# A norm and split emitted one output unit earlier, with its sum of squares pinned

## The chip, the cores and the metric

The kernel runs on one core of one Trainium2 chip. A core has a matrix engine (TensorE, PE in the profile; its weight loads are PEld), a vector engine (VectorE, DVE), a scalar engine for activations (ScalarE, ACT), GpSimd (POOL) and a queue engine that starts most transfers (SyncE, SP). Each engine works through its own queue in order, and engines wait for one another by semaphores. PE writes to eight accumulation banks (PSUM), which DVE and ACT read. The metric is the device time of one execution in microseconds.

## The reference

One inference step of a decoder trunk of one layer: a half-step SwiGLU feed-forward block, a mixer, a second such block, and a final norm, with plain residual adds. The input is one prompt of 512 tokens and 8 single new tokens of other sequences with saved state, each of 1024 features. The part around the change is the end of the mixer:

```python
y = y + d_skip[:, None] * xs_h
y = y.reshape(b, T, SSD_DIM) * jax.nn.silu(z)
yg = y.reshape(b, T, SSD_GROUPS, SSD_DIM // SSD_GROUPS)      # 2 groups of 512
yg = yg * lax.rsqrt(jnp.mean(yg * yg, axis=-1, keepdims=True) + EPS)
y = yg.reshape(b, T, SSD_DIM) * ssd_norm
cat = jnp.concatenate([pool_out, y], axis=-1)                # 512 + 1024
return cat @ w_out, ...
```

For the 8 new tokens, `y` also holds the product of the saved state with C, which comes from the sample stage below. The result of `cat @ w_out` is added to `h`, which feeds the norm and the gate and up projections of the second feed-forward block.

## The kernel before

Features lie on the 128 partitions, tokens along the free dimension: 520 of them (512 and 8), in two halves of 260. A big product is made of three matmuls for each tile of 128 features (`mm3`, L116 to L119): weight and input are each split into a rounded part (hi) and the rest (lo), and hi x hi, hi x lo and lo x hi are summed in a bank. The split of weights is a cast on ACT (L107, tile `whi`) and a subtraction on DVE (L108, tile `wlo`), three buffers each.

The mixer's order of emission is written out by hand in three strings, `CONV_PLAN`, `GATE_PLAN` and `LAST_PLAN`; each token names a stage and its argument. A planner then lays the emitted instructions out on the engines' queues: an instruction emitted earlier has the higher priority, but a later one may be put ahead of it where the planner holds the earlier one not ready. `tc.keep_in_program_order(x)` forbids one such move: `x` may not be put ahead of the instruction emitted just before it on the same engine. Buffers come from tags: all tiles of one tag share a fixed number of buffers. In the mixer all accumulation banks have one tag (`bank`, L76, eight buffers).

The stages that matter here, all in `mixer`:

- `s` (`sample`, L789): state product of one sequence and one group; loads two tiles through SP, then four products on DVE (L796, tile `junk`), kept in program order. There are 16.
- `G` (`gate`, L932): for group g, finishes the new tokens' part (L803, L804, L940), and multiplies `X` by the activated gate into `zs` (L942, four passes on DVE).
- `H` (`gate_out`, L944): the norm and split of group g. Four squares on ACT (L948, from `zs` into `X`), a sum over the features on PE by a matrix of ones (`rstd`, L158: four accumulating calls of L161 for each half of the tokens, tiles `psr_y{g}0` and `psr_y{g}1`, each in its bank), Sqrt on ACT (L162) and reciprocal on DVE (L163) for each half into `yr`; then four times a product on DVE (L955), a scaled copy on ACT (L956, hi part of `catg`) and a pass on DVE (L957, lo part).
- `o`, `g`, `h` (`wout`, L918): output units for the pooled input (`catp`), the first gate group (`cats[0]`) and the second (`cats[1]`). A unit is one weight load and split, 48 matmuls into four banks (12 each) and four evacuations on DVE that add to `h` (L926). Each letter has four units, 0 to 3.

Before the change H1 is emitted behind g1, the second unit of the first group; its product, `cats[1]`, is first read by h0, which is emitted behind g3. In the text H1, g0 to g3 and h0 stand for these stages.

An L161 call multiplies full fp32 numbers and shows as two PE instructions in the trace.

Of the kernel before, what the change touches and what calls it, by code (L numbers as in the profile page):

```python
# [41 lines left out]
)  # L42
GATE_PLAN = (
    "A4 z0 B3 z1 m3 z2 B4 z3 s2 A5 z4 s2 B5 A6 z5 s2 s2 G0 z6 A7 z7 B6 s2 o0 H0 s2 o1 B7 s2 o2 s2 G1 "
    "o3 g0 g1 H1 g2 g3"
)
LAST_PLAN = "h0 h2 h1 n0 h3 n1 n2 n3"
SAMPLE_U = 3 + SEQ
# [14 lines left out]
def tile_trunk_step(ctx: ExitStack, tc: tile.TileContext, ins: dict, outs: dict):  # L63
    nc = tc.nc

    def pool(name, side, **kw):
        return tc.alloc_tile_pool(name=name, bufs=1, side=side, reuse_waits="tile", **kw)
# [6 lines left out]
    ps = [None]  # L74

    def bank(name):  # L76
        return ps[0].tile([P, 512], F32, tag="ps", name=name)
# [8 lines left out]
    ones = cst.tile([P, P], F32, tag="ones", name="ones")  # L86
# [68 lines left out]
        nc.scalar.activation(out=sq, in_=h[:, d], func=AF.Square)  # L155
        nc.vector.tensor_tensor(out=nx[2], in0=nx[2], in1=sq, op=ALU.add)

    def rstd(r, acc, hs, width, name):  # L158
        ps = bank(f"psr_{name}")[:, : hs.stop - hs.start]
        for k, sq in enumerate(acc):  # L160
            nc.tensor.matmul(ps, ones, sq, start=k == 0, stop=k == len(acc) - 1)  # L161
        nc.scalar.activation(out=r[:, hs], in_=ps, func=AF.Sqrt, bias=eps, scale=1.0 / width)  # L162
        nc.vector.reciprocal(out=r[:, hs], in_=r[:, hs])  # L163

    def rstds(nx, name):
        for b, hs in enumerate(HALVES):
            rstd(nx[3], [nx[2][:, hs]], hs, D, f"{name}{b}")
# [270 lines left out]
    wx1, g1 = pool("wx1", "right"), pool("g1", "right")  # L438
# [4 lines left out]
    for j in range(KD // 2):  # L443
        for d in (j, j + KD // 2):
            q = slice(NVEC + d * NT if d else 0, NVEC + (d + 1) * NT)
# [62 lines left out]
    g2 = f2["ffn"].gp = pool("g2", "left")  # L508
# [52 lines left out]
def mixer(tc, ins, outs, e):  # L561
    nc = tc.nc
    cst, act, wp, tmp, dr, pool = (e[x] for x in ("cst", "act", "wp", "tmp", "dr", "pool"))
    ones = e["ones"]
    bank, load_unit, mm3, ws, v, rstd, rstds, vec, h, nx2, raw_tile, open_f2, fin, fill = (
        e[x] for x in ("bank", "load_unit", "mm3", "ws", "v", "rstd", "rstds", "vec", "h", "nx2", "raw_tile",
                       "open_f2", "fin", "fill"))
    xh, xl, _, r = nx2[0]
# [18 lines left out]
    X = mp.tile([P, NX, NT], F32, tag="X", name="X")  # L587
# [356 lines left out]
    def gate_out(g):  # L944
        zs = zbox[0]
        ry = mp.tile([P, NT], F32, tag="wph", name=f"yr{g}")
        for q in range(4):
            nc.scalar.activation(out=X[:, 4 * g + q], in_=zs[:, 4 * g + q], func=AF.Square)  # L948
        for b, hs in enumerate(HALVES):
            rstd(ry, [X[:, 4 * g + q, hs] for q in range(4)], hs, 512, f"y{g}{b}")  # L950
        cat = cats[g] = xa.tile([P, 2, 4, NT], F32R, tag="xa", bufs=2, name=f"catg{g}")
        for q in range(4):
            i = 4 * g + q
            gn = v("ssd_norm", i)
            nc.vector.tensor_tensor(out=zs[:, i], in0=zs[:, i], in1=ry, op=ALU.mult)  # L955
            nc.scalar.activation(out=cat[:, 0, q], in_=zs[:, i], func=AF.Copy, scale=gn)  # L956
            nc.vector.scalar_tensor_tensor(out=cat[:, 1, q], in0=zs[:, i], scalar=gn, in1=cat[:, 0, q].bitcast(F32),  # L957
                                           op0=ALU.mult, op1=ALU.subtract)
# [13 lines left out]
    def outs_a():  # L972
# [19 lines left out]
        "o": lambda j: wout(catp, 0, j),  # L992
        "G": gate,
        "H": gate_out,
        "g": lambda j: wout(cats[0], 1, j),
        "h": lambda j: wout(cats[1], 2, j, fin),
# [103 lines left out]
```

## Time and profile before

| what | value |
|---|---|
| median of 3 runs | 1002.59 us (1002.44 to 1002.99) |
| profiled execution, its own time | 1003.51 us |
| its span, first to last instruction | 1000.5 us |
| granted PE clock, mean over the span | 0.994 |
| g0 and g1 on PE (96 matmuls, `wo<-catg`) | 571.8 to 583.5 us |
| the four squares of group 1 on ACT (L948) | from 584.34, 2.61 us |
| calls of L161 for group 1 on PE | 585.03 to 591.3 us |
| first matmul of h0 on PE | 600.4 us |

Times in the trace are microseconds from the start of the span. A row of the timeline has start, duration, engine, line, operation, output tile and inputs, shapes and a count of merged instructions; in brackets, for how long the engine sat idle before it and which instruction ended that. In the list of waits, a row names the waiting engine, tile and line, whom it waited for, and the total, the number of times and the longest. Matmuls overlap by pipelining: their duration (0.28 us for 260 columns) is more than their distance in time (0.12 us).

### The profile page before, as it was taken

To read this page: it belongs to the slowest core of one execution; us is meant where nothing else is said; L and a number is where in the kernel's file an instruction comes from. 1 tells how busy PE (TensorE), PEld (TensorE's weight loads), DVE (VectorE), ACT (ScalarE), POOL (GpSimd) and SP (SyncE) were. 2 spreads that over 40 slices of the span, in tenths; PEclk is the share of its full clock that TensorE was granted. 3 is DMA by queue.
4 is the path that set the end of the run, shared out by engine and by line. 5 is a ranking of instruction groups with operands and counts; after the bars stand their busy time and mean duration, and the time that the engine had idled before them with its cause. 6 is when DMAs were issued, how large, how long until landed. Compare 5 with 4: busy or idle time off the path is not lost.

```text
span 1000.5 us, 19362 instructions
## 1 busy us (share of the span) xinstructions
PE 971.7 (97%) x7850; PEld 951.4 (95%) x7850; DVE 806.9 (81%) x1408; ACT 528.7 (53%) x881; POOL 87.8 (9%) x157
## 2 busy tenths in 40 slices
PE   7999999999999999999999999999999999999994
PEld 6899999999999999999899998899999999999993
DVE  7999657996569688788979987999957999668865
ACT  7566414664145455684845235666743666436552
POOL 0000000000000000167312000100012000120000
PEclk9999999999999999999999999999999999999997
DMA  6333232323223223263334421423346333452213
GB/s 194 112 126 114 98 101 73 124 88 124 85 85 106 85 104 117 87 216 105 107 133 122 146 90 54 124 94 118 127 137 187 120 127 118 124 195 96 95 33 85
DMA packets 44072, 114.44 MB, mean 114 GB/s; under 512 B 6408, under 2 KB 15560, under 8 KB 43984
## 3 DMA queue, kind: packets, MB, share of 16 engines
q1 hardware_dynamic: 40912, 103.78, 30.7%
q0 software_dynamic: 3072, 9.44, 3.5%
q8 instruction: 61, 1.00, 0.4%
q14 instruction: 27, 0.22, 0.1%
HBM read 105.86 MB, written 7.34 MB: 113 GB/s over the span
## 4 chain that ended last, share of the span: by engine, by line
PE 88%; DVE 6%; ACT 2%; POOL 2%; issue 1%; DMA 0%; SPq 0%; DVEq 0%; ACTq 0%
PE A L119 8%; PE A L117 8%; PE A L118 8%; PE dn L117 7%; PE dn L119 7%; PE dn L118 7%; PE BE L117 6%; PE BE L119 6%; PE BE L118 6%; PE P L232 4%; PE wo L117 2%; PE wo L118 2%; PE wo L119 2%; PE inz L117 2%; PE inz L119 2%; PE inz L118 2%
## 5 line engine op out<-in xcount | busy, mean ns | idle before, releaser
L117 PE MATMUL dn<-g,whi_1d 128*128 128x260 f32 x352 | 99.3, 283 | 0.2 <-DVE td L367 0.2
L118 PE MATMUL dn<-g,whi_1d 128*128 128x260 f32 x352 | 99.5, 283 | 0.0
L119 PE MATMUL dn<-g,wlo_1d 128*128 128x260 f32 x352 | 99.4, 283 | 0.0
L367 DVE SCALAR_TENSOR_TENSOR td<-dn,r_f 128x520 f32<-128x520 f32 x40 | 27.9, 699 | 73.2 <-PE dn L119 73.2
L119 PE MATMUL dn<-g,wlo_2d 128*128 128x260 f32 x256 | 72.4, 283 | 0.0
L118 PE MATMUL dn<-g,whi_2d 128*128 128x260 f32 x256 | 72.3, 282 | 0.0
L117 PE MATMUL dn<-g,whi_2d 128*128 128x260 f32 x256 | 72.3, 282 | 0.0
L117 PEld LDWEIGHTS dn<-g,whi_1d 128*128 128x128 f32 x352 | 66.1, 188 | 0.4 <-DVE td L367 0.4
L118 PEld LDWEIGHTS dn<-g,whi_1d 128*128 128x128 f32 x352 | 66.3, 188 | 0.0
L119 PEld LDWEIGHTS dn<-g,wlo_1d 128*128 128x128 f32 x352 | 66.2, 188 | 0.0
L297 ACT COPY ac<-A 128x260 f32<-128x260 f32 x123 | 45.6, 374 | 29.3 <-PE A L119 28.0
L107 ACT CAST whi_1d<-raw_1d 128x1024 fp32r<-128x1024 f32 (+1 forms) x24 | 23.4, 980 | 67.0 <-PE dn L118 54.2
L260 DVE TENSOR_TENSOR s<-raw 128x1024 f32<-128x1024 f32 x41 | 50.0, 1220 | 3.9 <-DMA raw<-in_w2gu 3.9
L232 PE MATMUL P<-xg_f,raw 128*128 128x260 f32 x192 | 45.1, 392 | 6.2 <-DMA raw<-in_w1gu 5.4
L232 PEld LDWEIGHTS P<-xg_f,raw 128*128 128x128 f32 x192 | 36.9, 195 | 12.1 <-ACT xg_f L179 5.4
L117 PEld LDWEIGHTS dn<-g,whi_2d 128*128 128x128 f32 x256 | 48.3, 189 | 0.0
L118 PEld LDWEIGHTS dn<-g,whi_2d 128*128 128x128 f32 x256 | 48.2, 188 | 0.0
L119 PEld LDWEIGHTS dn<-g,wlo_2d 128*128 128x128 f32 x256 | 48.2, 188 | 0.0
L118 PE MATMUL wo<-catg,whi_wo 128*128 128x260 f32 x128 | 36.4, 285 | 1.3 <-DVE catg L957 1.3
L117 PE MATMUL wo<-catg,whi_wo 128*128 128x260 f32 x128 | 37.3, 292 | 0.3 <-DVE h L926 0.3
L117 PE MATMUL inz<-xh_mx,whi_inz 128*128 128x260 f32 x128 | 36.8, 287 | 0.1
L117 PE MATMUL inx<-xh_mx,whi_inx 128*128 128x260 f32 x128 | 36.4, 284 | 0.0
(1340 smaller groups left out, 3924.1 us busy)
## 6 DMA issues: line engine op xcount, KB each, us to landing
raw<-in_w2gu SPq DMA_DIRECT2D x44, 512.0 KB, 4.5
raw<-in_w1gu SPq DMA_DIRECT2D x42, 512.0 KB, 4.4
raw_1d<-in_w1d SPq DMA_DIRECT2D x16, 512.0 KB, 4.4
raw_2d<-in_w2d SPq DMA_DIRECT2D x16, 512.0 KB, 4.6
raw_wo<-in_w_out SPq DMA_DIRECT2D x12, 512.0 KB, 5.0
ab<-scr_acs SPq DMA_DIRECT2D x8, 512.0 KB, 4.8
h<-in_state_ssm SPq DMA_DIRECT2D x16, 256.0 KB, 4.2
raw_inz<-in_w_in SPq DMA_DIRECT2D x8, 512.0 KB, 3.9
```

Of the source, the lines that this page charges most:

```text
L107: nc.scalar.copy(h, src)
L117: nc.tensor.matmul(ps, whi, xhi, start=start, stop=False, **kw)
L118: nc.tensor.matmul(ps, whi, xlo, start=False, stop=False, **kw)
L119: nc.tensor.matmul(ps, wlo, xhi, start=False, stop=stop, **kw)
L232: nc.tensor.matmul(self.banks[f, u][b][:, :HB], ws(self.raw[f][:, u], j + 4 * q), xg[:, slot[q]], start=j == q == 0, stop=j == 3 and q == ...
L260: nc.vector.tensor_tensor(out=s1, in0=diag, in1=up0, op=ALU.add)
L297: nc.scalar.copy(keep, out[:, :HB])
L367: nc.vector.scalar_tensor_tensor(out=t, in0=banks[d][:, :, :HB], scalar=-0.5, in1=self.nx[3].rearrange("p (b t) -> p b t", b=2), op0=ALU.mult,
```

## The change

H1 moves from behind g1 to behind g0 in the order of emission. In addition, for the second group alone, the first of the four accumulating calls in each half is pinned with `keep_in_program_order`. For the first half the instruction emitted just before it on PE is the last matmul of g0; for the second half it is the fourth call of the first half. What is computed stays the same.

```diff
 GATE_PLAN = (
     "A4 z0 B3 z1 m3 z2 B4 z3 s2 A5 z4 s2 B5 A6 z5 s2 s2 G0 z6 A7 z7 B6 s2 o0 H0 s2 o1 B7 s2 o2 s2 G1 "
-    "o3 g0 g1 H1 g2 g3"
+    "o3 g0 H1 g1 g2 g3"
 )
...
-    def rstd(r, acc, hs, width, name):
+    def rstd(r, acc, hs, width, name, pin=False):
         ps = bank(f"psr_{name}")[:, : hs.stop - hs.start]
         for k, sq in enumerate(acc):
-            nc.tensor.matmul(ps, ones, sq, start=k == 0, stop=k == len(acc) - 1)
+            m = nc.tensor.matmul(ps, ones, sq, start=k == 0, stop=k == len(acc) - 1)
+            if pin and k == 0:
+                tc.keep_in_program_order(m)
         nc.scalar.activation(out=r[:, hs], in_=ps, func=AF.Sqrt, bias=eps, scale=1.0 / width)
         nc.vector.reciprocal(out=r[:, hs], in_=r[:, hs])
...
         for b, hs in enumerate(HALVES):
-            rstd(ry, [X[:, 4 * g + q, hs] for q in range(4)], hs, 512, f"y{g}{b}")
+            rstd(ry, [X[:, 4 * g + q, hs] for q in range(4)], hs, 512, f"y{g}{b}", pin=g == 1)
```

## The prediction

> **What bounds the kernel now.** The page first: TensorE (PE) is busy nearly throughout, so a change pays or costs what it does to PE's gaps.
>
> ```profile
> PE 971.7 (97%) x7850; PEld 951.4 (95%) x7850; DVE 806.9 (81%) x1408; ACT 528.7 (53%) x881; POOL 87.8 (9%) x157
> ```
>
> Then the waits of PE from 380 to 660 us, and PE's busy time in four stretches around the moved step (busy us and number of matmuls, then the granted clock): unit g1; the second group's sum of squares (tile psr_y) with part of g2; the rest of g2, and g3; h0.
>
> ```profile
> PE psr_y L161 <- ACT X L948: 1.6, 1, 1.6
> PE wo L118 <- DVE catg L957: 1.3, 2, 0.6
> ...
> 577.40:583.20 5.80, 5.80 (x51) 1.00 0.42 141
> 583.20:591.30 8.10, 6.54 (x41) 1.00 0.08 33
> 591.30:600.20 8.90, 8.90 (x76) 1.00 0.25 83
> 600.20:608.60 8.40, 6.80 (x51) 1.00 0.10 41
> ```
>
> Two places have gaps: the sum of squares waits for the squares, and h0 for its input catg. g1, g2 and g3 run solid. Third, the timeline of PE there:
>
> ```profile
> 585.03 1.15 PE L161 MATMUL psr_y<-X,ones 128*128 128x260 f32 x4 [1.56 <-ACT X L948]
> ...
> 588.18 1.04 PE L161 MATMUL psr_y<-X,ones 128*128 128x260 f32 x4
> ...
> 589.30 1.04 PE L161 MATMUL psr_y<-X,ones 128*128 128x260 f32 x4
> ```
>
> Each row is two of the eight calls of L161 (two PE instructions a call), one for each half of the tokens; a fourth row follows at 590.30. Between the four rows stand 18, 2 and 1 matmuls of g2, which the planner slipped in. The reader is to see that nothing of g2 stands before the first row: PE idled 1.56 us, although g2's weights were split by 574.2 (the DVE row at 572.97 lasts 1.23) and at most two of the eight banks were still undrained. Fourth, what the squares wait for, on DVE and then ACT:
>
> ```profile
> 581.30 0.29 DVE L796 SCALAR_TENSOR_TENSOR junk<-h,cb 128x128 f32<-128x128 f32 x1
> ...
> 581.63 0.29 DVE L796 SCALAR_TENSOR_TENSOR junk<-h,cb 128x128 f32<-128x128 f32 x1
> ...
> 582.07 0.43 DVE L926 TENSOR_TENSOR h<-wo,h 128x260 f32<-128x260 f32 x1
> 582.41 0.18 DVE L803 TENSOR_TENSOR ysm<-ysm,sdec 128x32 f32<-128x32 f32 x1
> ...
> 583.42 0.70 DVE L942 TENSOR_TENSOR zs<-X,zs 128x520 f32<-128x520 f32 x1
> 584.03 0.42 DVE L926 TENSOR_TENSOR h<-wo,h 128x260 f32<-128x260 f32 x1
> 584.36 1.91 DVE L942 TENSOR_TENSOR zs<-X,zs 128x520 f32<-128x520 f32 x3
> ...
> 584.34 2.61 ACT L948 ACTIVATE X<-zs 128x520 f32<-128x520 f32 x4
> ```
>
> The second group's gate (L803 to L942) starts when the last sample product (L796) is done, at 581.9, more than 4 us after g0's last matmul (577.5). The change moves neither. Last, how the planner hands out buffers of one tag, on POOL:
>
> ```profile
> 370.77 0.20 POOL L683 COPY U<-sconv 128x24 f32<-128x24 f32 x1 [13.00 <-DMA sconv<-in_state_conv]
> 378.03 0.19 POOL L694 COPY ncp<-U 128x3 f32<-128x3 f32 x1 [7.06 <-DVE U L603]
> ...
> 378.33 0.10 POOL L681 MEMSET U<- 128x3 f32 x1
> ```
>
> The memset opens the second convolution's U and needs no data, and the tag has six buffers. Yet it is queued behind a copy that had to wait 7.06 us for the first U, beside the first write of the tile emitted in between (A, ACT L688, 378.38). So buffers of a tag seem to be given in the order of emission, even when later ones are free. The bank tag agrees: psr_y's two banks are emitted ahead of g2's, and g2 did not begin before both were opened.
>
> **The change part by part.** It removes and adds no instruction. H1 issues on PE 8 calls, on ACT 4 squares, 2 Sqrt and 4 copies, on DVE 2 reciprocals and 8 passes of zs and catg; no DMA, and nothing on SP or POOL. It passes g1: the weight load and split, 48 matmuls and four evacuations. g1's load and split are through before any of H1 is ready, so only matmuls and evacuations can change place.
>
> *Step 1, what holds g1.* psr_y's two banks now come ahead of g1's. By the rule above g1 cannot open its first bank until both psr_y banks are opened. The pin puts the first call of the second half behind the call before it on PE, which is the fourth call of the first half. So g1 waits until all four squares are done. Queued behind the wait are g1, g2 and g3, all of PE's work; the pin on the first half costs nothing, since its call is late anyway.
>
> *Step 2, when the squares are done.* g1's first three evacuations no longer stand on DVE between the last samples. From 579.84 five sample products remain, at 0.33 (581.30 to 581.63): the last at 581.16. The step from the last one to L803 is 0.34 in the first group (538.71 to 539.05), so L803 starts at 581.5 instead of 582.41. The first L942 comes 1.01 later as now, 582.5, and four at 0.61 end at 585.0. A square of 0.64 ends at 585.7. Bounds: 584.5 if the weight split on DVE (1.23) also falls behind the samples, and 586.95 as now if nothing is won; 585.7 is from the rows nearest to it.
>
> *Step 3, PE around it.* A call takes 0.44 (pitch 0.22 an instruction). Fourth call of the first half: to 586.15; four of the second half: to 587.9. In the profile g1 starts at 577.54 (g0 starts at 571.77, 48 matmuls at 0.120). So 10.4 us without output matmuls, 3.5 of them the calls. Today's cost is from g1's end (583.31) to the last psr_y call (590.99), 7.68, less 21 matmuls of g2 (2.53): 5.15. Net +5.25.
>
> *Step 4, h0.* Its 48 matmuls run from 600.37 to 608.72, 8.35 against 5.77 unhindered, so it stalls 2.6. From the second Sqrt to the last catg pass is 13.2 now (591.4 to 604.6). From some 589 on it ends near 602, and h0 cannot start before 587.9 + 144 x 0.120 = 605.2. The stall goes: -2.6. Next late is nothing on DVE; PE itself is. Evacuations of g1 behind the two reciprocals (1.78 each) cost nothing while other banks are free; without that cover up to 1.5.
>
> *Step 5, PE's clock.* An idle time of 6.3 us (577.54 to 583.84, the first square's end) is far longer than any in the middle of this trace. Its nearest rows are at the ends:
>
> ```profile
> 5.44 4.26 PE L232 MATMUL P<-xg_f,raw 128*128 128x260 f32 x12 [5.44 <-DMA raw<-in_w1gu]
> ...
> 987.76 1.14 PE L543 MATMUL psl<-acc_last,ones 128*128 128x260 f32 x2 [2.89 <-DVE acc_last L148]
> ...
> 988.00:1000.00 12.00, 1.77 (x4) 0.84 (x3) 4.46 (x6) 0.48 (x1) 0.00 (x0) 0.50 0.43 89
> ```
>
> After 2.89 us idle the granted clock is 0.50. At the start the same shape as psr_y's took 0.43 a piece until the clock rose at 8.27, 2.83 us after the first. So I expect half clock from 583.84 for 2.83 us. In it 3.25 calls of 0.87 get done; at full clock, partly waiting for squares, 5.25 would have been: 2 calls, +0.9. Ends: nothing, if the clock stays (1.56 idle left it at 1.00), and +3.0 if all eight calls run at half clock (583.84 + 6.96 = 590.8 against 587.9). I take 0.9, from the start of this program.
> [...]
>
> *Sum.* +5.25 - 2.6 + 0.9 = +3.5 us. From h0 on PE is solid up to a wait of 1.37 on ACT's copy of PE's own result (643.97), which moves along and absorbs nothing. The profiled execution took 1003.51 (span 1000.5, 3.0 around it): 1007.0. The median is 0.92 below it, so 1002.59 + 3.5 = **1006.1**.
>
> **The rivals.** *Faster: g1 and g2 are not held.* If the planner places a call whenever its square is ready and fills with output matmuls, the 1.56 idle goes, and the calls need not come 18 matmuls late: Sqrt near 587.5 instead of 590.94, the last catg pass near 601.1. h0 would start at 598.8 and stall 1.5 of today's 2.6. Gain 1.6 + 1.1 = 2.7: **999.9**. It decides if g1's matmuls run on from 577.5. For it: matmuls were slipped in between later calls. Against it: none was slipped in before the first, and the memset.
>
> *No change.* If the order stays as it was because nothing of H1 is ready before g1 ends: **1002.6**. For it: the gate ends at 583 either way. Against it: the same bank order.
>
> *The clock stays half for all eight calls:* the upper end of step 5, **1008.2**. For it: the calls come sparsely at first, with squares 0.61 apart. Against it: at half clock a call of 0.87 fills that pitch, so PE is busy throughout, as at the start. [...]
>
> **How the numbers follow.** Chances: forecast 0.68, long half clock 0.12, faster rival 0.12, no change 0.08. The forecast's own range is 1004.0 (squares at 584.5, no clock loss: +1.4) to 1007.5 (squares 1.2 later, with 0.9 of clock: +4.8). The range given runs from the no-change case with its spread, 1002.3, to the long half clock with 0.6 on top, 1008.8, and leaves out the faster rival and tails. Measurement tells about 0.2% (2.0 us) from no change: below 1000.6 is faster, above 1004.6 slower. Faster 0.12; same 0.08 plus 0.05 of the forecast's low end, 0.13; slower 0.75.
>
> **What would show it.** Step 1: no wo matmul between 577.5 and the first psr_y call, and psr_y's calls in one row after it. Step 2: L803 near 581.5, the fourth square ending near 585.7. Steps 3 and 4: a wait of PE for ACT L948 of about 6 us, and no wait of wo for catg. Step 5: a granted clock below 1.00 from some 581 to 587, and calls of 0.87. The prediction is wrong if g1's matmuls precede the calls, or if DVE finishes the samples well before 581.

## The result and the profile after

The change makes the kernel slower by 0.39%: 1006.69 us (median of six runs, 1006.12 to 1007.32) against 1002.79 us (six, 1001.8 to 1003.54), a ratio of 1.0039 with a 95% interval of 1.0026 to 1.0052. The profiled execution took 1006.12 us (before: 1003.51), its span is 1004.2 us (1000.5) and its mean granted clock 0.991 (0.994). Lines behind L161 stand two lower in the new file: L948 is now L950, L803 is L805.

First the waits of PE from 560 to 660 us in the kernel after (engine, tile and line, whom it waited for; total us, times, longest):

```profile
PE psr_y L161 <- ACT X L950: 6.2, 1, 6.2
PE A L117 <- ACT ac L299: 1.8, 2, 1.4
```

The sum of squares now waits 6.2 us for the squares, where it waited 1.6; the wait of h0 for catg (1.3 us) is gone. The wait of A is far behind and was there before. The timeline of PE in the kernel after shows the place:

```profile
583.53 5.36 PE L161 MATMUL psr_y<-X,ones 128*128 128x260 f32 x16 [6.22 <-ACT X L950]
...
588.53 0.47 PE L117 MATMUL wo<-catg,whi_wo 128*128 128x260 f32 x1
```

All eight calls (16 instructions) stand in one row, and the first matmul of g1 opens behind them, 11.22 us after the end of g0 (577.31). PE in four stretches of the kernel after, with its busy time, its matmuls and the granted clock: idle, half clock, the rest of the calls, and g1 to the end of h0:

```profile
577.31:579.94 2.63, 0.00 (x0) 1.00 0.03 6
579.94:586.77 6.83, 3.24 (x8) 0.50 0.44 154
586.77:588.50 1.73, 1.73 (x9) 1.00 0.00 0
588.50:611.98 23.48, 23.48 (x195) 1.00 0.13 46
```

The clock halved while PE was idle and stayed at half for 3.24 us after PE had resumed; then g1, g2, g3 and h0 ran without a gap. What the squares wait for, on DVE in the kernel after:

```profile
580.78 0.29 DVE L798 SCALAR_TENSOR_TENSOR junk<-h,cb 128x128 f32<-128x128 f32 x1
...
581.11 0.19 DVE L805 TENSOR_TENSOR ysm<-ysm,sdec 128x32 f32<-128x32 f32 x1
...
582.12 2.52 DVE L944 TENSOR_TENSOR zs<-X,zs 128x520 f32<-128x520 f32 x4
```

and the squares themselves on ACT:

```profile
582.84 2.47 ACT L950 ACTIVATE X<-zs 128x520 f32<-128x520 f32 x4 [4.57 <-DVE zs L944]
```

The gate starts behind the last sample product as before, and the fourth square ends at 585.31, 1.64 us earlier than before the change (586.95), or 1.25 earlier counted from the start of g0.

For what follows one yardstick is used beside the total: the *stretch* from the first matmul of g0 to the last matmul of h0 on PE, 240 output matmuls and the eight calls, in the one profiled execution of each kernel. It was 36.99 us before (571.76 to 608.75) and is **40.60** after (571.38 to 611.98): +3.61. Its terms before were 1.56 of waiting for squares, about 3.5 for the calls, and a stall of about 2.6 in h0; after they are 6.22 of waiting, 5.0 for the calls (583.53 to 588.53) and no stall: +4.7 + 1.5 - 2.6 = +3.6. g0 itself started 0.39 earlier, so h0 ended 3.23 later. The other 392 us behind it are 0.5 us longer, with one wait in them that the profile of before does not have:

```profile
PE dn L119 <- DVE wlo_2d L108: 1.1, 1, 1.1
```

It goes back to a tile of gate and up weights of the second block that was issued at 886.2 and kept DVE waiting 3.87 us until 894.38, 8.2 us later. Before the change the same tile was used 6.2 us after its issue (882.95 to 889.10); the median of such transfers is 4.5. Waits of PE of this kind come to 1.8 us in two of the profiles below (e4_kept_busy, e11_inside_g1_busy), to 0.2 to 0.6 in three (e7_own_banks_late, e9_inside_g1, e12_inside_g2_no_pin) and to nothing in the others, so they add to the totals; whether they come by chance isn't known. The stretch leaves them out, but it stands for one execution.

### The profile page after: what moved, and what is told of

Same layout as the page of the kernel before. It is cut to its first block, busy times and chain, and to the rows that moved or that the text cites. A ratio compares the mean times of both kernels' runs of the same rounds, so it can differ in the third digit from the quotient of the medians.

```text
span 1004.2 us, 19363 instructions
## 1 busy us (share of the span) xinstructions
PE 972.9 (97%) x7850; PEld 952.8 (95%) x7850; DVE 808.8 (81%) x1408; ACT 528.4 (53%) x881; POOL 85.7 (9%) x157
## 4 chain that ended last, share of the span: by engine, by line
PE 88%; DVE 5%; ACT 2%; issue 1%; POOL 1%; DMA 1%; DVEq 0%; SPq 0%; ACTq 0%
PE A L119 8%; PE A L117 8%; PE A L118 8%; PE dn L119 7%; PE dn L117 7%; PE dn L118 7%; PE BE L117 6%; PE BE L119 6%; PE BE L118 6%; PE P L234 4%; PE wo L117 2%; PE wo L119 2%; PE wo L118 2%; PE inz L117 2%; PE inz L119 2%; PE inz L118 2%
## 5 line engine op out<-in xcount | busy, mean ns | idle before, releaser
L234 PE MATMUL P<-xg_f,raw 128*128 128x260 f32 x192 | 46.1, 398 | 5.1 <-ACT xg_f L181 5.1
L234 PEld LDWEIGHTS P<-xg_f,raw 128*128 128x128 f32 x192 | 37.5, 199 | 11.1 <-ACT xg_f L181 5.1
L117 PE MATMUL wo<-catg,whi_wo 128*128 128x260 f32 x128 | 37.2, 291 | 0.0
L119 PE MATMUL wo<-catg,wlo_wo 128*128 128x260 f32 x128 | 36.2, 283 | 0.0
```

The costliest lines, as they stand in the source:

```text
L117: nc.tensor.matmul(ps, whi, xhi, start=start, stop=False, **kw)
L119: nc.tensor.matmul(ps, wlo, xhi, start=False, stop=stop, **kw)
L234: nc.tensor.matmul(self.banks[f, u][b][:, :HB], ws(self.raw[f][:, u], j + 4 * q), xg[:, slot[q]], start=j == q == 0, stop=j == 3 and q == ...
```

## The experiments

The theory: the time is lost where PE stands still for the squares, because psr_y's two banks are handed out ahead of g1's; the place of H1 in the order sets for how long, and the half clock adds about 1 us. Rivals: the pin, not the place, holds PE; or what is lost is the clock and not the standing still. "Before" was run again beside each set: 1003.88, 1003.91 and 1003.87 us.

**e1_no_pin: the new place without the pin.**

```diff
-            rstd(ry, [...], hs, 512, f"y{g}{b}", pin=g == 1)
+            rstd(ry, [...], hs, 512, f"y{g}{b}")
```

> H1 behind g0 as in the changed kernel, without the pin. Theory (psr_y's banks are given out ahead of g1's, so g1 waits for the calls that open them; the idle time then halves the clock): g1 now waits only for the first call of each half, that is for the first square. PE still idles about 6.2 us from g0's end, the first two calls run at half clock (1.7 us), and g1 opens near 585.3 instead of 588.5; but some 15 of its matmuls run at half clock (0.24 instead of 0.12) and the other six calls come later in one or more groups. Sum: 6.2 idle + 3.5 calls + 1.65 of half clock + 0.2 for one more switch, 0.3 more than in the changed kernel: 1006.5 to 1007.5. Rival (the pin is what costs): the wait for the second to fourth square and the clock go, and the time falls by 2 us or more, to 1004.5 or less.

Measured: 1007.66 us, ratio 1.0035 (1.0023 to 1.0046), stretch 41.17. The rows of psr_y in its timeline of PE:

```profile
584.65 2.10 PE L161 MATMUL psr_y<-X,ones 128*128 128x260 f32 x4 [6.23 <-ACT X L950]
...
589.55 2.79 PE L161 MATMUL psr_y<-X,ones 128*128 128x260 f32 x12
```

The same idle time without a pin. Once the first call of each half has run (four instructions), 15 matmuls of g1 go ahead of the other six calls: once both banks are opened g1 may start, but not sooner. So the loss is not the pin's. g1 opens 7.8 us after g0's end (8.0 was expected), and the total is 0.2 above the range that was expected.

**e2_pin_old_place: the pin alone, H1 behind g1 as before.**

```diff
-    "o3 g0 H1 g1 g2 g3"
+    "o3 g0 g1 H1 g2 g3"
```

> The pin alone, with H1 behind g1 as before. Theory: the eight calls stand in one row between g1 and g2, PE waits for all four squares there (from 583.3 to 585.0 for the first, and calls until some 589.2: 5.9 us without output matmuls where the kernel before has 5.15), but Sqrt of the first half comes at 587.5 instead of 590.9, catg is ready 2 to 3 us earlier and h0's stall of 2.6 goes: 0.75 - 2.6 = -1.85 us, about 1000.9, clock at 1.00 throughout. Rival (the pin costs by itself, wherever H1 stands): 1 us or more above before, 1003.8.

Measured: 1001.49 us, ratio 0.9974 (0.9965 to 0.9984): **faster** than before. The calls come in one row, as the timeline of PE shows, and h0 no longer waits:

```profile
585.78 5.91 PE L161 MATMUL psr_y<-X,ones 128*128 128x260 f32 x16 [1.56 <-ACT X L950]
```

The idle time before them is that of before, to the hundredth; so the place, not the pin, sets it, and of the two parts of the change the pin gains and the move loses. The stretch of the profiled execution is 36.56, only 0.43 less than before, while the total is 2.4 less. This execution lost part of its gain to the clock, as its busy time of PE in two windows shows (busy us, matmuls, clock):

```profile
584.00:587.00 3.00, 1.40 (x6) 1.00 0.25 100
587.20:590.50 3.30, 3.30 (x9) 0.50 0.03 5
```

After 1.56 us of idle time and calls at the pace of the squares, the clock fell to half for 3.41 us. The expectation had the clock at 1.00 throughout. The mean granted clock is near 0.995 in about half of the twelve executions and near 0.993, as here, in the others, so about half probably had no such time at half clock. By an estimate from the calls (5.91 us here, 4.29 at full clock in e4_kept_busy below) that is worth up to 1.6 us in one execution and about 1 us of the 2 in the median. What the rest is stays open; the executions of the kernel before also differ in clock (0.991 to 0.995).

**e3_own_banks: the change, with two banks of the mixer's eight set aside for psr_y.**

```diff
     def bank(name):
-        return ps[0].tile([P, 512], F32, tag="ps", name=name)
+        if name.startswith("psr_y"):
+            return ps[0].tile([P, 512], F32, tag="pr", bufs=2, name=name)
+        return ps[0].tile([P, 512], F32, tag="ps", bufs=ps[1], name=name)     # ps[1]: 6 in the mixer
```

> The changed kernel with two banks of their own (a tag of its own) for psr_y, and six instead of eight for the rest of the mixer. Theory: nothing holds g1 then; g1's and part of g2's matmuls run on from g0's end, the calls come only where the planner holds the squares ready, PE has no wait for L950 above 0.5 us, the clock stays at 1.00, and h0 waits for catg again for 2 to 4 us: 1002 to 1004, near the kernel before. Rival (the earlier place of H1 on the queues of DVE and ACT costs, not the banks): it stays near 1006.7.

Measured: 1006.9 us, ratio 1.0029 (1.0019 to 1.004). The total misses: six banks are too few for the mixer's earlier stages, which waited 2.0, 0.5 and 0.9 us between 476 and 494 and lost the full clock for 3.41 us there (from 480.05; mean granted clock of the profiled execution 0.990), and g0 started at 575.31 instead of 571.4. The stretch answers the question nevertheless: no wait at psr_y, g1 running on from g0, 37.47 against 40.60, with 2.7 us of waits for catg in h0. In h0 the expectation of a clock at 1.00 failed too: it was at half for 3.41 us from 606.35.

**e7_own_banks_late: the same, but six and two from g0 on only, and for the second group alone.**

```diff
-    "o3 g0 H1 g1 g2 g3"
+    "o3 S0 g0 H1 g1 g2 g3"
...
+    def six_and_two(j):              # stage S: a new pool of banks
+        ps[0].release()
+        ps[0] = tc.alloc_tile_pool(name="ppo", bufs=8, space=PSUM, reuse_waits="tile")
+        ps[1] = 6
```

with `bank` as in e3_own_banks for `psr_y1`.

> The changed kernel, with psr_y's two banks of the second group in a tag of their own from g0 on (six banks for the output units), and all eight in one tag until then, so that the stages before are as they were. Measured from g0's first to h0's last matmul, the kernel before takes 37.0 us and the changed one 40.6. Theory (the order in which banks are given out holds g1): g1 and part of g2 run on without a wait, the calls come some 10 us after g0's end, h0 waits for catg 2 to 3 us, and the stretch takes 37 to 38: about 0.5 us above before in all. Rival (the earlier place of H1 costs by itself): the stretch stays at 40 to 41, in all 3.5 us above before.

Measured: 1001.78 us, ratio 0.9982 (0.9973 to 0.9991), stretch 35.87. Its waits of PE (H's lines stand higher by some in this file):

```profile
PE wo L120 <- DVE catg L963: 2.1, 2, 1.3
...
PE wo L119 <- DVE h L932: 0.3, 1, 0.3
```

No wait for the squares is left. The first call stands in the timeline of PE as

```profile
587.13 0.60 PE L163 MATMUL psr_y<-X,ones 128*128 128x260 f32 x2
```

From the start of g0, 130 output matmuls run before it, although the place of H1 and the pin are those of the change (the last square is done 14.79 us after the start of g0, 13.93 in the change). This shows that the banks' order held g1, and that the pin by itself does not. What comes next is h0 again: the calls now start 15.64 us after g0's first matmul, later than in any other kernel but e3_own_banks (15.76) and e10_behind_g2 (17.31), and h0 waits for catg. The stretch is 1 us shorter than was expected; unlike e3_own_banks, this execution kept the full clock in h0.

**e4_kept_busy: the change, with 50 matmuls between g0 and the calls whose result nobody reads.**

```diff
+        if g == 1:
+            dm = bank("dm")
+            for k in range(50):
+                m = nc.tensor.matmul(dm[:, :HB], ws(catp[:, 0, 0], 0), catp[:, 1, 0, :HB], start=k == 0, stop=k == 49)
+                tc.keep_in_program_order(m)
         for b, hs in enumerate(HALVES):
```

> The changed kernel with 50 more matmuls (128x260, 0.12 us each, 6 us) between g0 and psr_y, of a result that nobody reads, so that PE is not idle while it waits. Theory: the granted clock stays at 1.00, a call takes 0.44 instead of up to 0.87, and g1 opens about 1.0 us earlier against g0's end (10.2 us after it instead of 11.2): 1005.7. Rival (half the clock costs nothing, since the calls wait for the squares anyway): g1 opens 11.2 us after g0's end and the time stays at 1006.7. Third case (the upper end of the clock's price): 3 us less, 1003.7.

Measured: 1008.12 us, ratio 1.0037 (1.0023 to 1.0052); stretch 39.58. Its timeline of PE:

```profile
578.16 6.17 PE L954 MATMUL dm<-catp 128*128 128x260 f32 x50
584.57 4.29 PE L161 MATMUL psr_y<-X,ones 128*128 128x260 f32 x16 [0.24 <-ACT X L950]
```

The clock stays at 1.00 throughout, the calls take 4.29 instead of 5.36, and g1 opens 10.18 us after g0's end instead of 11.22. So, by the stretch, the half clock costs about 1.0 of the 3.6 us, and the standing still the rest. The totals do not confirm this 1 us: the change is 0.39% and this kernel 0.37% above the runs of before beside them, which is 0.2 us apart, and the 1005.7 that was expected is missed by 2.4. In this profile g0 starts 1.01 us later than in that of the change, the stretch is 1.02 shorter and what follows it is 2.1 longer. Waits for late transfers explain 0.8 of the 2.1 (1.85 us against 1.1); the other 1.3 is not explained.

**e9_inside_g1, e8_inside_g2, e10_behind_g2: other places, with the pin.** The first two emit H1 in the middle of a unit, between its two tiles of features:

```diff
-    def wout(cat, j, d2, fin=None):
+    def wout(cat, j, d2, fin=None, mid=None):
...
+            if mid is not None and d == 2 * d2:
+                mid()
...
-        "g": lambda j: wout(cats[0], 1, j),
+        "g": lambda j: wout(cats[0], 1, j, mid=(lambda: gate_out(1)) if j == 2 else None),   # e9: j == 1
```

with "o3 g0 g1 g2 g3" as the end of the plan; the third has "o3 g0 g1 g2 H1 g3".

> H1 with its pin in the middle of g1, behind its first 24 matmuls, 2.9 us of work later than in the changed kernel. Theory: the wait of PE falls by those 2.9 us, from 6.2 to some 3.3; the clock halves in most executions for one window; no wait of h0. The stretch from g0's first to h0's last matmul takes about 37.5 (changed kernel 40.6): 0 to 1 us above before in all. Rival (the halved clock and not the wait is what costs): little change from the changed kernel as long as the clock halves, 3 us above before.

> H1 with its pin emitted in the middle of g2, behind its first 24 matmuls. Theory (what PE pays is the time from the place of the calls to the squares): the squares are done when PE comes to the calls, so PE has no wait for L950 above 0.3 us and no half clock, the eight calls take 3.9 us in one row, catg is ready when h0 starts or up to 0.5 us later. From g0's first to h0's last matmul: 240 matmuls 28.9, calls 3.9, tail and rest 0.3 to 0.8, so 33.1 to 33.6 where before takes 37.0: 3.5 us below before in all, and 1 us or more below the pin at the old place. Rival (the later Sqrt makes h0 wait for catg again): no gain on the pin at the old place, 2.5 us below before or less.

> H1 with its pin behind the whole of g2. Theory: no wait at the calls, 3.9 us in one row, but the second Sqrt comes 2.9 us of work later than with H1 inside g2, and h0 waits for catg for 1 to 2.5 us. The stretch takes 34.5 to 36: 1 to 2.5 us below before in all. Rival (catg is early enough in any case): as with H1 inside g2, 3.5 us below before.

Measured, in order of place ("ahead" are the output matmuls between the start of g0 and the calls; idle is PE's wait for the squares, "half clock" how long the granted clock was at half, h0 PE's waits in h0):

| place of H1 (with the pin) | ahead | idle | half clock | h0 | stretch | ratio to before (95%) |
|---|---|---|---|---|---|---|
| behind g0 (the change) | 48 | 6.22 | 6.83 | 0 | 40.60 | 1.0039 (1.0026 to 1.0052) |
| in g1 (e9) | 72 | 3.80 | 6.83 | 0 | 39.56 | 1.0017 (1.0009 to 1.0026) |
| behind g1 (e2) | 96 | 1.56 | 3.41 | 0 | 36.56 | 0.9974 (0.9965 to 0.9984) |
| in g2 (e8) | 120 | 0 | 0 | 0 | **33.34** | **0.9967 (0.9955 to 0.998)** |
| behind g2 (e10) | 144 | 0 | 0 | 1.1 | 34.42 | 0.9977 (0.9966 to 0.9987) |

In the middle of g2 nothing is left: the only waits of PE from 560 to 660 us in that kernel are

```profile
PE A L117 <- ACT ac L299: 1.8, 2, 1.4
PE BE L117 <- ACT ac L299: 0.2, 1, 0.2
```

and in its timeline of PE the calls are

```profile
587.04 3.67 PE L161 MATMUL psr_y<-X,ones 128*128 128x260 f32 x16
```

The calls start 14.43 us after the start of g0, behind 120 matmuls at 0.120. In this trace the first square is done 13.21 us after the start of g0 and the fourth 15.18; the calls follow one another at 0.44, so the fourth call needs the fourth square at about 15.75. (In the change the squares are done 12.10 to 13.93 us after the start of g0; here, as before the change, g1's first evacuations stand between the last samples and the gate's passes on DVE.) So the calls stand where they can just run, at full clock and without a pause. The kernel takes 1000.59 us, faster than both kernels, with the stretch that was expected. Half a unit earlier PE waits for the squares (1.56 us), half a unit later h0 waits for the norm (1.1). The ratios of the last three rows overlap within their intervals, so that this is the best place is shown by the stretch alone. e10_behind_g2 lies just below its expectation; e9_inside_g1 is 2 us off, and its timeline and PE's windows say why:

```profile
584.84 6.70 PE L161 MATMUL psr_y<-X,ones 128*128 128x260 f32 x16 [3.80 <-ACT X L952]
```

```profile
583.90:590.80 6.90, 5.96 (x14) 0.51 0.07 30
```

The clock was at half from 583.97 to 590.80, 6.83 us, through nearly all of the calls. "One window" in the expectation is a time at half clock like the 3.41 us in e2_pin_old_place; the run had twice that.

**e11_inside_g1_busy: e9_inside_g1 with 30 unused matmuls ahead of the calls,** which separates its clock from its idle time. The edit is that of e4_kept_busy with 30 for 50.

> H1 with its pin inside g1 as in the last but one run, with 30 more matmuls of a result that nobody reads (3.6 us) ahead of its calls, so that PE does not idle while it waits. There the stretch from g0's first to h0's last matmul took 39.56 us, 2 us above what was expected, with half clock for 6.83 us. Theory (all of that excess is the clock: every call at 0.87): at full clock the last call ends 16.6 us after g0's first matmul instead of 19.3, and the stretch takes 36.6 to 37.2, some 2.6 us less; in all 0 to 0.5 us below before. Rival (the clock costs the 0.9 us of the prediction, the rest is a later square): 38.5 to 38.9, in all 1.5 above before.

Measured: 1003.87 us, ratio 1.0003 (0.9992 to 1.0014), stretch 37.15. Its row of psr_y:

```profile
584.31 4.29 PE L161 MATMUL psr_y<-X,ones 128*128 128x260 f32 x16 [0.20 <-ACT X L952]
```

4.29 instead of 6.70: the half clock had cost 2.4 us there, more than twice what it cost in the change, although PE had stood idle for a shorter time. The wait itself is no shorter; the matmuls only filled it. The medians are 1.5 us apart and not 2.4; this profile has 1.8 us of waits for late transfers where that of e9_inside_g1 has 0.2.

**e12_inside_g2_no_pin: the best place without the pin.** The edit is that of e8_inside_g2, with `pin=g == 1` dropped.

> H1 in the middle of g2 without the pin. With it the stretch from g0's first to h0's last matmul took 33.34 us. Theory (the pin of the second half is what keeps the eight calls in one row): the first call of each half comes at the same place, then 15 matmuls of g2, then the other six; the last call ends about 2 us later, catg too, and h0 waits again: 34.2 to 35 us, in all 2 to 3 us below before. Rival (the place alone matters): 33.3 to 33.6 as with the pin.

Measured: 1004.87 us, ratio 1.0014 (1.0005 to 1.0023), stretch 37.57 instead of 33.34. Its psr_y rows and its waits of PE from 560 to 660 us:

```profile
586.59 1.04 PE L161 MATMUL psr_y<-X,ones 128*128 128x260 f32 x4
...
589.26 2.79 PE L161 MATMUL psr_y<-X,ones 128*128 128x260 f32 x12
```

```profile
PE wo L117 <- DVE h L928: 1.6, 2, 1.4
PE wo L118 <- DVE catg L961: 1.0, 2, 0.6
```

The planner runs the first call of each half, puts 15 matmuls of g2 between, and ends the calls 1.8 us later (19.90 against 18.10 us from the start of g0). h0 then waits 2.6 us, and the clock was at half for 3.41 us from 601.75. The expectation was too small by some 3 us: only the later calls had been counted, not h0's order, which the planner also changed (its second matmul opens another bank and waits 1.36 us for an evacuation on DVE), nor the clock.

## Why the prediction was right

The median is 1006.69 where 1006.1 was forecast, slower as forecast, and for the reasons given; the steps one by one:

- *Step 1 (what holds g1): right.* No output matmul stands between 577.31 and the calls, and these are in one row. That the banks' order does it, read from a memset on POOL, is shown by e7_own_banks_late. That the pin costs nothing on the first half fits e1_no_pin, where the wait is the same without it. That the pin's second half makes g1 wait for all four squares fits too: without it g1 opens 7.8 us after g0's end instead of 11.2, but the calls end later, and the stretch is no shorter (41.17).
- *Step 2 (when the squares are done): right.* L805 at 581.11 (581.5 forecast), the last square at 585.31 (585.7); both are 0.4 early because g0 started 0.39 earlier in this trace.
- *Step 3 (PE around it): right.* 6.22 us idle (6.3) and no output matmul for 11.22 us, against 10.4 plus 0.9 for the clock. With the clock held up, e4_kept_busy measured 10.18 for the 10.4.
- *Step 4 (h0's stall): right in what it decided, wrong in a size.* The stall is gone and PE runs solid from g1 to the end of h0. But catg was ready at 597.6 (the last pass, two at 596.20 for 1.42), not "near 602": from the second Sqrt (588.93) it took 8.7 us, and the 13.2 of before was carried over unexamined. (h0's first matmul in the profile before starts at 600.21, not 600.37; its stall is 2.6 either way.) It made no difference with h0 starting after 605; it would have if H1 had been placed later, where h0 does wait.
- *Step 5 (the clock): the cost right partly by luck, the start and the length wrong.* The half clock lasted 6.83 us, from 579.94 to 586.77, and not 2.83 from the first call. It began while PE was still idle, so that only 3.24 us of it met any work, and it cost 1.0 by e4_kept_busy, where 0.9 was forecast. Two errors cancelled: the half clock lasted longer than forecast, and more of it lay over idle time. Where it falls could not be told from the pause, as the last section shows; in e9_inside_g1 half clock of the same length cost 2.4. The row from the start of the program showed only the end of a time at the slow pace, and with it no length: 2.8 us before, 4.8 in the profile after.
- *The rivals.* g1's matmuls did not run on, and the order did not stay. The half clock was long in the change, but over half of it met no work; in e9_inside_g1 it met nearly all of the calls, at 2.4 of the 3.0 us that this rival was priced at.
- *The sum.* +5.25 - 2.6 + 0.9 = +3.55 forecast; the stretch measured +3.61 and the medians +3.9, of which the late transfer in the profile may be a part; for the other executions this isn't known.

## What to carry to other kernels

With this planner, an instruction that opens a buffer of a shared tag holds everything that is emitted later under that tag (PE stood idle for 6.22 us here, and did not wait for the squares with banks of their own in e7_own_banks_late). So a step whose input is late should be emitted at the point where its input arrives, counted in work of the engine that would wait: here 120 matmuls of 0.120 us, 14.4 us, against 13.2 to 15.2 us until the four squares are done, one after the other. The middle of a unit hits that and neither of its ends does. Move and pin are to be tried apart: here the pin was worth 0.26% at the old place and about 4 us of stretch at the best one, while the move, with the pin at both places, cost 0.65%. And where totals scatter by two microseconds, a stretch between two fixed instructions in the trace tells what a change did in that execution, without what happens elsewhere.

## What the runs showed of the hardware

- In the middle of the traces the granted clock was at half for 6.83 us in the change (579.94 to 586.77) and e9_inside_g1 (583.97 to 590.80), and for 3.41 us in e2_pin_old_place (from 587.11), e12_inside_g2_no_pin (from 601.75) and twice in e3_own_banks (from 480.05 and 606.35). In e1_no_pin the matmuls of g1 came 0.22 us apart, and not 0.12, until 589.1.
- At the start of the program the matmuls of L232 (L234 after the change) came at two paces: in the profile before, 7 in the 2.81 us from 5.44 to 8.25 and 55 in the 11.70 from 8.30 to 20 (0.40 and 0.21 us each); in the profile after, 11 in the 4.79 us from 5.11 to 9.90 and 47 in the 10.05 from 9.95 to 20 (0.44 and 0.21). So the slow pace, which the prediction took for half clock, lasted 2.8 us behind the first matmul in one and 4.8 in the other.
- In these traces the start of the half clock isn't tied to the pause or to the first matmul behind it. The fall came 2.6 us after PE fell idle in the change, and in e2_pin_old_place 1.3 us *after* PE had resumed from a pause of only 1.56 us with calls at the pace of the squares; the same pause in the profile before left the clock at 1.00. What sets it stays open.
- What it costs depends on what falls into it: 1.0 us in the change, where half of it lay over idle time, and 2.4 in e9_inside_g1 with 2.4 us less idle time. So a pause of 3.80 us on PE cost more in clock here than one of 6.22.
